# The backward key transposes of a head go to the PSUM bank of the head outputs

## The chip, the cores and the metric

The kernel runs on one core of a Trainium2 chip. The metric is the device time of one execution in microseconds (us); lower is better. Three runs of the kernel before took 1967.69, 1967.95 and 1969.16 us, so the median is 1967.95 us.

Engines are named as the profile names them: PE is the matmul engine (PEld its weight loads), DVE the vector engine, ACT the scalar engine, POOL the GpSimd engine, SP the engine that issues most DMAs. Each engine works through its own instructions in the order of the program and stands still at an instruction that has to wait for another engine.

## The reference

The reference is one layer of a bidirectional encoder over 1024 positions of width 1024, all in float32: a mixer branch with 8 heads (HGRN2, a gated linear recurrence, run forward and backward in time), a gated spatial branch, a merge of the two, and then a gated feed-forward layer and a gated residual. What matters here is the recurrence of one head and one direction:

```
def step(state, inp):
    qc, kc, vc, gc = inp                       # one chunk of positions
    b = jnp.cumsum(gc, axis=2)
    o_inter = jnp.einsum('bhtk,bhkv->bhtv', qc * jnp.exp(b), state)
    ...
    scores = jnp.einsum('bhtk,bhsk,bhtsk->bhts', qc, kc, decay)
    o_intra = jnp.einsum('bhts,bhsv->bhtv', scores, vc)
    new_state = exp(b_last) * state + einsum('bhsk,bhsv->bhkv', kc * exp(b_last - b), vc)
    return new_state, o_inter + o_intra
```

Both directions run over the same queries and values, and their outputs are added, normalised per head and gated.

## The kernel before, in words

The kernel splits the 1024 positions into 8 chunks of 128. For each of the 8 heads it does three things.

`proj` makes the forget gates and keys of a head from the normalised input, with matmuls of 512 columns in line 133 (`mm3`) that write the banks `ps_mm`. These are long and wait for little: they fill PE while a head's chains run elsewhere.

`scores` builds the score matrices of a head in seven levels, for blocks of m = 1, 2, 4, ... 64 positions, after a first product in line 613. At each level line 624 multiplies the decayed keys `X` with the decayed queries `QA` (four matmuls for each half of the positions, into a bank `ps_sc`), DVE updates `QA` (line 633) and the next `X` (line 636), line 646 or 643 merges the bank into the scores `SC`, ACT copies the middle of the next `X` from `Y` (line 657), POOL makes the next `Y` from `X` (line 660), and DVE halves the number of gate factors `F` (line 666). A level's `X` is a new tile; three buffers rotate, so the third level of a head overwrites the last `X` of the head before, and has to wait for those who still read it.

`outputs` takes the last `X` and `Y` of a head, which are the keys decayed to their chunk's borders. For two groups of chunks (4 and 3 of the 7 that pass a state on) and for both directions d (0 forward, 1 backward) it transposes the keys on PE (line 683) into a PSUM bank, copies them on ACT to the tile `kt` (line 685), multiplies them with the values (line 688, bank `ps_st`, of which there is one), and adds the products to the running states `S` on DVE (lines 692 and 694). Then line 712 computes the head's outputs into the bank `ps_o`, and line 722 transposes them into `ps_tr`.

PSUM has eight banks, given out by tags: three `mm`, two `sc`, and one each of `tr`, `st` and `o` (`PS_BUFS`, line 56). A bank that is to be written again waits until its last reader is done. Before the change all key transposes of heads 0 to 6 go to the one bank `tr`, so each of the four groups waits until ACT has copied the group before it. In the last head the backward ones go to `sc`, which is free by then.

The program is written head by head as `scores(h)`, `proj(h+1)`, `outputs(h)`, but that isn't the order in which it runs: a scheduler with a model of the engines' times sorts the instructions of each engine (`schedule_with_timeline_sim`, line 1090). So the end of the levels of head h, the transposes and states of head h, and the first levels of head h+1 are mixed on each engine. The prediction calls this stretch the passage from head h to head h+1. In the traced execution the passage from head 2 to head 3 lies at about 722 to 741 us.

Of the kernel before, what the change touches and what calls it, by code (L numbers as in the profile page):

```python
# [22 lines left out]
H = 8  # L23
# [12 lines left out]
def kernel(ctx: ExitStack, tc: tile.TileContext, a: dict, out: bass.AP):  # L36
# [18 lines left out]
    def ps_tile(tag):  # L55
        return psum.tile([P, NH], F32, name=f"ps_{tag}", tag=tag, bufs=PS_BUFS[tag])
# [16 lines left out]
    def t2(pool, role, bufs=2):  # L73
        return pool.tile([P, NH], F32, name=role, tag=role, bufs=bufs)

    def sm(role, w=1):
        return small.tile([P, w], F32, name=role, tag=role)
# [18 lines left out]
    def rstd_from(role, ssq, w, scale):  # L96

        v = sm(role + "v", w)
        nc.vector.tensor_scalar(out=v, in0=ssq, scalar1=scale, scalar2=EPS, op0=ALU.mult, op1=ALU.add)
        r = sm(role + "r", w)  # L100
        nc.gpsimd.tensor_tensor(out=r, in0=v, in1=expo[:, 0:w], op=ALU.pow)
        return r
# [10 lines left out]
    def split_into(hi, lo, src, eng=None):  # L113
        nc.scalar.activation(hi, src, AF.Copy)  # L114
        (eng or nc.vector).tensor_tensor(out=lo, in0=src, in1=hi.bitcast(F32), op=ALU.subtract)  # L115
# [339 lines left out]
    for t in range(NT):  # L455
        tp = ps_tile(("tr", "o")[t % 2])
# [213 lines left out]
    def outputs(h, s):  # L670
        QA, SC, X, Y, F, v = s.QA, s.SC, s.X, s.Y, s.F, s.v

        S = hg.tile([P, 2, NT - 1, P], F32, name="S")
        orders = [list(range(NT - 1)), list(range(NT - 1, 0, -1))]
        prev = [None, None]
        for g0 in range(0, NT - 1, 4):
            for d in range(2):
                cs = orders[d][g0:g0 + 4]
                n = len(cs)
                tp = ps_tile("sc" if h == H - 1 and d else "tr")  # L680
                for i, c in enumerate(cs):
                    src = X if c % 2 == d else Y
                    nc.tensor.transpose(tp[:, i * P:(i + 1) * P], src[:, c * P:(c + 1) * P], ident)
                kt = hg.tile([P, 4, P], F32, name="kt", bufs=2)
                nc.scalar.activation(kt[:, 0:n], tp[:, 0:n * P].rearrange("p (c t) -> p c t", c=n), AF.Copy)
                up = ps_tile("sc" if h == H - 1 and d else "st")
                for i, c in enumerate(cs):
                    nc.tensor.matmul(up[:, i * P:(i + 1) * P], lhsT=kt[:, i], rhs=v[:, c], start=True, stop=True)  # L688
                for i, c in enumerate(cs):
                    uv = up[:, i * P:(i + 1) * P]  # L690
                    if prev[d] is None:
                        nc.vector.tensor_copy(S[:, d, c - d], uv)
                    else:
                        nc.vector.scalar_tensor_tensor(
                            out=S[:, d, c - d], in0=S[:, d, prev[d] - d], scalar=F[:, 1 - d, c:c + 1], in1=uv,
                            op0=ALU.mult, op1=ALU.add)
                    prev[d] = c


        for g in range(2):  # L700
            op = ps_tile("sc" if h == H - 1 and g else "o")
            ssq = sm("os", 4)
            for i in range(4):
                c = 4 * g + i
                cs = slice(c * P, (c + 1) * P)
                terms = [(SC[:, c], v[:, c])]
                if c > 0:
                    terms.append((QA[:, 1, cs], S[:, 0, c - 1]))
                if c < NT - 1:
                    terms.append((QA[:, 0, cs], S[:, 1, c]))  # L710
                for j, (l, r) in enumerate(terms):
                    nc.tensor.matmul(op[:, i * P:(i + 1) * P], lhsT=l, rhs=r, start=(j == 0), stop=(j == len(terms) - 1))  # L712
            on = t2(t1, "on")
            for i in range(4):
                nc.scalar.activation(on[:, i * P:(i + 1) * P], op[:, i * P:(i + 1) * P], AF.Square,
                                     accum_out=ssq[:, i:i + 1])
            r = rstd_from("o", ssq, 4, 1.0 / P)
            for i in range(4):
                nc.scalar.activation(on[:, i * P:(i + 1) * P], op[:, i * P:(i + 1) * P], AF.Identity, scale=r[:, i:i + 1])
            tp = ps_tile("tr")  # L720
            for i in range(4):
                nc.tensor.transpose(tp[:, i * P:(i + 1) * P], on[:, i * P:(i + 1) * P], ident)
            gs = slice(g * NH, (g + 1) * NH)
            nc.vector.scalar_tensor_tensor(out=on, in0=tp, scalar=vec[:, 2, h:h + 1], in1=s.zg[:, gs],
                                           op0=ALU.mult, op1=ALU.mult)
            if h == H - 1:
                A = (A0, A1)[g]
                split_into(A[0][1][:, h % 4, :], A[1][1][:, h % 4, :], on)
            else:
                nc.sync.dma_start(at_d[h, :, gs], on)  # L730
# [28 lines left out]
    for h in range(H):  # L759
        nxt = Head()  # L760
        scores(h, cur)
        if h + 1 < H:
            proj(nxt, h + 1, "qfbg")
        if h == H - 1:

            gate_a(0)
            A0 = new_fm("A0")
            load_A(0, A0, range(H - 1), 5)
            gate_a(1)
            A1 = new_fm("A1")  # L770
            wa = [split_wa(load_wa(j)) for j in range(2)]
        outputs(h, cur)
        cur = nxt
# [320 lines left out]
```

## Time and profile before

| what | value |
|---|---|
| median of three runs | 1967.95 us |
| profiled execution, its own time | 1966.99 us |
| span of the profiled execution | 1965.2 us |
| PE busy | 1910.8 us, 97% of the span |
| DVE, ACT, POOL busy | 1120.0, 757.2, 206.7 us |
| share of PE in the chain that ended last | 90% |

The profiled execution was about 1 us shorter than the median. Times in the rows below are counted from the start of the span. PE is busy almost everywhere, so a shorter or longer time comes from the places where it stands idle. A row of the timeline merges equal instructions that follow each other on an engine; a float32 matmul of 128 columns appears as two.

### The profile page before, as it was taken

What the parts mean: (1) busy time and instruction counts of PE and PEld (TensorE: products, weight loads), DVE (VectorE), ACT (ScalarE), POOL (GpSimd) and SP (SyncE); (2) the same over time, 40 slices, a digit from 0 to 9 for tenths busy, and PEclk for the clock granted to TensorE, in tenths of its full rate; (3) what the DMA queues carried; (4) which work ended last, traced back from release to release, by engine and by line L of the source; (5) the groups of instructions that cost most, each with busy time, mean ns of one, the idle gap of its engine ahead of it and who ended that gap; (6) DMA issues with size and microseconds to landing.
All of it is one profiled execution on the core that took longest, in us unless ns stands there. A gap on an engine that the chain in (4) does not pass through costs nothing.

```text
span 1965.2 us, 24005 instructions
## 1 busy us (share of the span) xinstructions
PE 1910.8 (97%) x9264; PEld 1596.0 (81%) x9264; DVE 1120.0 (57%) x1712; ACT 757.2 (39%) x1424; POOL 206.7 (11%) x153
## 2 busy tenths in 40 slices
PE   7999999999999999999989998999999999999999
PEld 6887888888887888888877887888888888888887
DVE  7402385544348777777665468855554537545743
ACT  6312254343354545545441356433333324112321
POOL 2600000000012222222112100000000000001000
PEclk9999999999999999999999999999999999999999
DMA  7220245323231221212336333232222106315222
GB/s 292 93 88 27 87 172 170 130 105 110 86 123 33 70 71 63 66 55 68 126 106 208 107 99 103 97 112 78 89 76 86 65 33 209 108 65 163 92 102 79
DMA packets 82690, 201.86 MB, mean 103 GB/s; under 512 B 8720, under 2 KB 18064, under 8 KB 82576
## 3 DMA queue, kind: packets, MB, share of 16 engines
q1 hardware_dynamic: 82576, 200.33, 30.2%
q8 instruction: 73, 1.20, 0.3%
q14 instruction: 41, 0.34, 0.0%
HBM read 147.35 MB, written 52.95 MB: 102 GB/s over the span
## 4 chain that ended last, share of the span: by engine, by line
PE 90%; DVE 4%; ACT 2%; DMA 2%; POOL 1%; issue 1%; SPq 0%; DVEq 0%; POOLq 0%; ACTq 0%
PE ps_mm L133 29%; PE ps_mm L278 20%; PE ps_sc L133 11%; PE ps_sc L278 10%; PE ps_st L133 6%; PE ps_sc L624 4%; PE ps_o L278 2%; PE ps_o L712 2%; PE ps_tr L278 2%; PE ps_st L278 1%; DVE QA L633 1%; POOL Y L660 1%; PE ps_st L688 1%; ACT SC L643 0%; DMA raw<-in_w_gate_dram 0%
## 5 line engine op out<-in xcount | busy, mean ns | idle before, releaser
L278 PE MATMUL ps_mm<-T,w 128*128 128x512 f32 x1296 | 309.6, 389 | 0.0
L278 PEld LDWEIGHTS ps_mm<-T,w 128*128 128x128 f32 x1296 | 243.2, 188 | 50.7 <-ACT u L228 0.2
L115 DVE TENSOR_TENSOR whl<-raw,whl 128x1024 fp32r<-128x1024 f32 (+1 forms) x70 | 89.6, 1282 | 142.7 <-ACT whl L114 142.6
L660 POOL TENSOR_TENSOR Y<-X,F 128x512 f32<-128x512 f32 x56 | 92.4, 1651 | 696.1 <-DVE F L599 392.4
L624 PE MATMUL ps_sc<-QA,X 128*128 128x128 f32 x896 | 126.4, 288 | 16.9 <-DVE QA L633 16.9
L115 DVE TENSOR_TENSOR w<-sums,w 128x1024 fp32r<-128x1024 f32 x72 | 88.0, 1223 | 94.2 <-ACT w L114 94.2
L624 PEld LDWEIGHTS ps_sc<-QA,X 128*128 128x128 f32 x896 | 116.1, 192 | 26.1 <-DVE QA L633 19.0
L133 PE MATMUL ps_mm<-whl,act 128*128 128x512 f32 x528 | 134.1, 389 | 0.0
L114 ACT ACTIVATE whl<-raw 128x1024 fp32r<-128x1024 f32 (+1 forms) x78 | 79.1, 1017 | 120.2 <-PE ps_sc L133 52.4
L633 DVE TENSOR_TENSOR QA<-QA,F 128x512 f32<-128x512 f32 x112 | 91.8, 828 | 49.2 <-PE ps_sc L624 48.1
L133 PE MATMUL ps_mm<-hTb,whl 128*128 128x512 f32 x480 | 118.6, 396 | 0.0
L133 PEld LDWEIGHTS ps_mm<-whl,act 128*128 128x128 f32 x528 | 99.1, 188 | 20.7
L133 PE MATMUL ps_mm<-hTa,whl 128*128 128x512 f32 x480 | 115.1, 392 | 0.0
L114 ACT ACTIVATE w<-sums 128x1024 fp32r<-128x1024 f32 x72 | 75.9, 1055 | 99.9 <-PE ps_sc L278 76.9
L278 PE MATMUL ps_sc<-T,w 128*128 128x512 f32 x432 | 107.5, 389 | 0.0
L133 PEld LDWEIGHTS ps_mm<-hTa,whl 128*128 128x128 f32 x480 | 89.4, 188 | 18.1
L133 PEld LDWEIGHTS ps_mm<-hTb,whl 128*128 128x128 f32 x480 | 88.2, 188 | 16.8
L278 PEld LDWEIGHTS ps_sc<-T,w 128*128 128x128 f32 x432 | 81.1, 188 | 16.9
L133 PE MATMUL ps_sc<-whl,act 128*128 128x512 f32 x354 | 91.0, 390 | 0.3 <-ACT acc L953 0.3
L133 PEld LDWEIGHTS ps_sc<-whl,act 128*128 128x128 f32 x354 | 66.3, 188 | 14.3 <-ACT acc L953 0.7
L115 POOL TENSOR_TENSOR wpg<-raw,wpg 128x1024 fp32r<-128x1024 f32 x4 | 9.6, 2403 | 598.3 <-ACT wpg L114 593.6
L278 PE MATMUL ps_mm<-B,wA 128*128 128x512 f32 x264 | 67.3, 399 | 1.7 <-ACT wA L114 1.7
(309 smaller groups left out, 3574.2 us busy)
## 6 DMA issues: line engine op xcount, KB each, us to landing
raw<-in_w_fm_dram SPq DMA_DIRECT2D x52, 512.0 KB, 3.6
raw<-in_w_gate_dram SPq DMA_DIRECT2D x22, 512.0 KB, 3.4
raw<-in_w_up_dram SPq DMA_DIRECT2D x22, 512.0 KB, 3.9
act_d<-s SPq DMA_DIRECT2D x22, 512.0 KB, 2.8
raw<-in_w_down_dram SPq DMA_DIRECT2D x22, 512.0 KB, 4.4
raw<-act_d SPq DMA_DIRECT2D x22, 512.0 KB, 4.2
raw<-in_w_tm_dram SPq DMA_DIRECT2D x16, 512.0 KB, 4.1
pr_d<-vs SPq DMA_DIRECT2D x16, 256.0 KB, 5.9
```

The costliest lines, as they stand in the source:

```text
L114: nc.scalar.activation(hi, src, AF.Copy)
L115: (eng or nc.vector).tensor_tensor(out=lo, in0=src, in1=hi.bitcast(F32), op=ALU.subtract)
L133: nc.tensor.matmul(ps, lhsT=lhs(lp, k), rhs=rhs(rp, k), start=(i == 0), stop=(i == n - 1))
L278: nc.tensor.matmul(ps, lhsT=lhs(lp, k), rhs=rhs(rp, k), start=(first and i == 0), stop=(i == n - 1), skip_group_check=True)
L624: nc.tensor.matmul(sp[:, i * P:(i + 1) * P], lhsT=X[:, c * P:(c + 1) * P], rhs=view(QA, c * P, [[2 * m, cb], [T + m, 2], [1, m]]), start=T ...
L633: nc.vector.tensor_tensor(out=view(QA, o, qd), in0=view(QA, o, qd), in1=view(F, of + 1, [[nb - 1, 2], [2, nb // 4], [0, m]]), op=ALU.mult)
L660: nc.gpsimd.tensor_tensor(out=view(Y, m, mid), in0=view(X, m, mid), in1=view(F, 0, [[4, nb // 4], [nb + 3, 2], [0, m]]), op=ALU.mult)
L688: nc.tensor.matmul(up[:, i * P:(i + 1) * P], lhsT=kt[:, i], rhs=v[:, c], start=True, stop=True)
L712: nc.tensor.matmul(op[:, i * P:(i + 1) * P], lhsT=l, rhs=r, start=(j == 0), stop=(j == len(terms) - 1))
```

## The change

One line of `outputs` picks the bank of the key transposes by direction. The forward transposes stay in `tr`; the backward ones go to `o`, or in the last head to `sc` as before.

```
@@ -677,7 +677,7 @@
             for d in range(2):
                 cs = orders[d][g0:g0 + 4]
                 n = len(cs)
-                tp = ps_tile("sc" if h == H - 1 and d else "tr")
+                tp = ps_tile(("tr", "sc" if h == H - 1 else "o")[d])
                 for i, c in enumerate(cs):
                     src = X if c % 2 == d else Y
                     nc.tensor.transpose(tp[:, i * P:(i + 1) * P], src[:, c * P:(c + 1) * P], ident)
```

No instruction is added or removed, but the scheduler puts many of them elsewhere. On PE, in the passage from head 2 to head 3, from the second half of the product of line 613 (`ps_sc_5409`) to the first level of head 3 (`ps_sc_5416` and `ps_sc_5424` are its two halves), this is the order before:

```order
L613 MATMUL ps_sc_5409<-q_5126,ks_5399 128x128 [waits PE_49,Activation_49]
L613 MATMUL ps_sc_5409<-q_5126,ks_5399 128x128 x3
L683 MATMUL ps_tr_5306<-ident_79,X_5103 128x128 [waits Activation_49]
L683 MATMUL ps_tr_5306<-ident_79,Y_4686 128x128
L683 MATMUL ps_tr_5306<-ident_79,X_5103 128x128
L688 MATMUL ps_st_5297<-v_4827,kt_5295 128x128 [waits DVE_49]
L688 MATMUL ps_st_5297<-v_4827,kt_5295 128x128 x3
L624 MATMUL ps_sc_5416<-QA_5398,X0_5129 128x128 [waits Activation_49]
L624 MATMUL ps_sc_5416<-QA_5398,X0_5129 128x128 x3
L683 MATMUL ps_tr_5319<-ident_79,X_5103 128x128 [waits Activation_49]
L683 MATMUL ps_tr_5319<-ident_79,Y_4686 128x128
L683 MATMUL ps_tr_5319<-ident_79,X_5103 128x128
```

And this is the order now, at the same place:

```order
L613 MATMUL ps_sc_5409<-q_5126,ks_5399 128x128 [waits PE_49,Activation_49]
L613 MATMUL ps_sc_5409<-q_5126,ks_5399 128x128 x3
L688 MATMUL ps_st_5297<-v_4827,kt_5295 128x128 [waits DVE_49]
L688 MATMUL ps_st_5297<-v_4827,kt_5295 128x128 x3
L624 MATMUL ps_sc_5416<-QA_5398,X0_5129 128x128 [waits Activation_49]
L624 MATMUL ps_sc_5416<-QA_5398,X0_5129 128x128 x3
L712 MATMUL ps_o_5332<-v_4827,SC_4956 128x128 [waits Activation_49]
L624 MATMUL ps_sc_5424<-QA_5398,X0_5129 128x128 [waits DVE_49]
L624 MATMUL ps_sc_5424<-QA_5398,X0_5129 128x128 x3
```

The six transposes that stood among these matmuls now stand ahead of line 613, and the first matmul of line 712, which needs the bank `o` free again, has moved behind the first half of the level. What is left between line 613 and the first level is the state product `ps_st_5297`, which waits for DVE.

On DVE, at the same passage, the order before is this (`X_5436` and `X_5457` are the second and third new `X` of head 3, `ps_st_5281` the first state product of head 2):

```order
L636 TENSOR_TENSOR X_5436<-X_5415,F2_5434 128x64x2x2 [waits DVE_49]
L666 TENSOR_TENSOR F64_5545<-F32_5518 128x32 [waits DVE_49]
L692 COPY S_5273<-ps_st_5281 128x128 [waits PE_49]
L666 TENSOR_TENSOR F128_5568<-F64_5545 128x16 [waits DVE_49]
L694 SCALAR_TENSOR_TENSOR S_5273<-S_5273,F128_5124,ps_st_5281 128x128 [waits DVE_49] x3
L692 COPY S_5273<-ps_st_5297 128x128 [waits PE_49]
```

And this is the order now:

```order
L636 TENSOR_TENSOR X_5436<-X_5415,F2_5434 128x64x2x2 [waits DVE_49]
L666 TENSOR_TENSOR F64_5545<-F32_5518 128x32 [waits DVE_49]
L692 COPY S_5273<-ps_st_5281 128x128 [waits PE_49]
L636 TENSOR_TENSOR X_5457<-X_5436,F4_5455 128x32x2x4 [waits DVE_49,PE_49,Activation_49]
L636 TENSOR_TENSOR X_5457<-X_5436,F4_5455 128x32x2x4 [waits DVE_49]
L666 TENSOR_TENSOR F128_5568<-F64_5545 128x16 [waits DVE_49]
L694 SCALAR_TENSOR_TENSOR S_5273<-S_5273,F128_5124,ps_st_5281 128x128 [waits DVE_49] x3
L692 COPY S_5273<-ps_st_5297 128x128 [waits PE_49]
```

The pair of line 636 that makes the third `X` of the next head has moved from behind the first update of `QA` (line 633, further down) to ahead of the three state updates of line 694. It reads `X_5436`, whose middle ACT writes (line 657). On ACT the second copy `kt` of a head now follows the first at once, the fourth has moved behind the two copies of line 614, and so has line 657 of the third level moved ahead of them. POOL's and SP's orders are the same. These moves are the same at the passages from heads 0 to 5; at the passage from head 6 to head 7, where the last projection matmuls lie between the levels, they are spread over a longer stretch.

## Rows read from the trace of the kernel before

**Rows 1.** The page's first line.

```profile
span 1965.2 us, 24005 instructions
```

**Rows 2.** Waits on PE, 610 to 1025 us: waiter, releaser, total us, times, longest.

```profile
PE ps_tr L683 <- ACT kt L685: 6.5, 5, 1.3
```

**Rows 3.** Timeline, 718 to 742 us: start, length, engine, line, operation, [idle before <-releaser].

```profile
727.19 4.13 POOL L660 TENSOR_TENSOR Y<-X,F 128x512 f32<-128x512 f32 x1 [3.37 <-ACT X L657]
...
728.87 0.75 DVE L636 TENSOR_TENSOR X<-X,F 128x256 f32<-128x256 f32 x2
...
729.35 1.87 PEld L613 LDWEIGHTS ps_sc<-q,ks 128*128 128x128 f32 x16
...
729.54 1.83 DVE L666 TENSOR_TENSOR F<-F 128x32 f32<-128x32 f32 x1
731.29 0.28 DVE L692 COPY S<-ps_st 128x128 f32<-128x128 f32 x1
731.35 0.67 ACT L657 ACTIVATE X<-Y 128x512 f32<-128x512 f32 x1 [2.17 <-POOL Y L660]
...
731.61 1.11 DVE L694 SCALAR_TENSOR_TENSOR S<-S,F,ps_st 128x128 f32<-128x128 f32 x3
732.04 0.60 ACT L685 ACTIVATE kt<-ps_tr 128x512 f32<-128x512 f32 x1
732.10 1.50 POOL L660 TENSOR_TENSOR Y<-X,F 128x512 f32<-128x512 f32 x1 [0.78 <-ACT X L657]
...
732.69 0.14 PEld L683 LDWEIGHTS ps_tr<-ident,X 128*128 128x128 f32 x1 [1.47 <-ACT kt L685]
...
732.97 0.97 PEld L688 LDWEIGHTS ps_st<-v,kt 128*128 128x128 f32 x8
...
733.86 1.29 PEld L624 LDWEIGHTS ps_sc<-QA,X 128*128 128x128 f32 x8
...
735.50 0.69 DVE L633 TENSOR_TENSOR QA<-QA,F 128x512 f32<-128x512 f32 x1 [0.27 <-PE ps_sc L624]
...
736.24 1.28 PEld L624 LDWEIGHTS ps_sc<-QA,X 128*128 128x128 f32 x8 [0.70 <-DVE QA L633]
...
737.64 1.27 POOL L660 TENSOR_TENSOR Y<-X,F 128x512 f32<-128x512 f32 x1 [4.05 <-ACT X L657]
...
737.87 1.59 DVE L633 TENSOR_TENSOR QA<-QA,F 128x512 f32<-128x512 f32 x1
...
739.52 1.02 PEld L624 LDWEIGHTS ps_sc<-QA,X 128*128 128x128 f32 x8 [1.21 <-DVE QA L633]
...
740.47 1.69 PEld L133 LDWEIGHTS ps_mm<-hTb,whl 128*128 128x128 f32 x8
```

**Rows 4.** Timeline of POOL, 660 to 900 us: first and last of five like this.

```profile
674.33 4.13 POOL L660 TENSOR_TENSOR Y<-X,F 128x512 f32<-128x512 f32 x1 [3.36 <-ACT X L657]
...
885.74 4.20 POOL L660 TENSOR_TENSOR Y<-X,F 128x512 f32<-128x512 f32 x1 [3.36 <-ACT X L657]
```

**Rows 5.** Timeline, 620 to 635 us, the passage from head 0 to head 1.

```profile
624.01 1.80 POOL L660 TENSOR_TENSOR Y<-X,F 128x512 f32<-128x512 f32 x1 [0.79 <-ACT X L657]
624.37 1.49 DVE L666 TENSOR_TENSOR F<-F 128x32 f32<-128x32 f32 x1
...
627.26 0.97 PEld L688 LDWEIGHTS ps_st<-v,kt 128*128 128x128 f32 x8 [1.84 <-DVE S L694]
```

**Rows 6.** Timeline of PEld at three other places with long idle times.

```profile
34.36 1.23 PEld L133 LDWEIGHTS ps_mm<-wp,pT 128*128 128x128 f32 x6 [2.40 <-DVE vs L405]
...
1017.86 0.91 PEld L722 LDWEIGHTS ps_tr<-ident,on 128*128 128x128 f32 x4 [3.11 <-ACT on L719]
...
1209.27 0.42 PEld L846 LDWEIGHTS ps_tr<-ident,y 128*128 128x128 f32 x4 [3.21 <-issue]
```

**Rows 7.** Windows: stretch, us, busy of PE, PEld, DVE, ACT, POOL, granted clock, DMA.

```profile
1019.60:1022.90 3.30, 3.00 (x9) 2.57 (x10) 2.44 (x5) 1.65 (x4) 0.00 (x0) 0.50 0.00 0
...
1210.70:1217.40 6.70, 5.32 (x12) 3.92 (x13) 5.93 (x9) 5.16 (x12) 0.00 (x0) 0.50 0.30 85
```

More of the change, by code (lines that the diff above doesn't have):

```diff
@@ L679, in outputs @@
                 n = len(cs)
-                tp = ps_tile("sc" if h == H - 1 and d else "tr")
+                tp = ps_tile(("tr", "sc" if h == H - 1 else "o")[d])
                 for i, c in enumerate(cs):
```

## The prediction

> **What bounds the kernel now.** I read the page first. The span is 1965.2 us [rows 1] and PE is busy nearly all of it, so only PE's idle places can change the time. Next I read the waits of PE over the heads. The wait that the change aims at is there: a transpose of line 683 waits for ACT's copy to `kt`, 5 times, 6.5 us in all, never above 1.3 us [rows 2]. Those five are the passages from heads 1 to 5. Last I read the timeline of one passage, from head 2 to head 3, engine by engine [rows 3].
>
> The chain in it runs like this. POOL's op of line 660 is issued at 727.19 and takes 4.13 us. DVE works without a pause beside it until 729.62 (the pair of line 636), and then DVE's next op, a tiny one of line 666, takes 1.83 us; both end together, at 731.32 and 731.37. ACT's copy of line 657 needs that `Y` and starts at 731.35. Behind it in ACT's order stands the second copy to `kt`, at 732.04. PE has been through with line 613 since about 731.14 (two loads per 0.223 us, 16 loads from 729.35) and stands until 732.69, when the bank `tr` is free. Then come three transposes, the state product (732.97), the first half of the next head's first level (733.86), DVE's update of `QA` (735.50), the second half (736.24), the second update (737.87 to 739.46) and the first half of the second level (739.52). From 740.47 the long matmuls of line 133 run and PE has no more such gaps until the next passage. So a delay of the matmul at 739.52 is a delay of the whole program, once per passage.
>
> **What the change takes away.** The third and fourth group of transposes no longer wait for ACT's second `kt`, which now stands ahead of POOL's long op. They go into the idle time ahead of line 613; ten transposes at some 0.11 us are hidden there and cost nothing. If nothing else stood in the way, the state product could follow line 613 at 731.14, where it starts at 732.97: at most 1.83 us per passage, 9.2 us over five.
>
> **What is late next.** The state product writes the only bank `st`, and has to wait for the three updates of line 694 that read the product before. In the trace these run 731.61 to 732.72, right behind lines 692 and 666. In the new order the pair of line 636 stands between, and that pair reads the `X` whose middle ACT writes at 731.35 to 732.02. DVE, with everything behind it, waits for that copy:
>
> - the pair starts at about 732.05 and takes 0.75, as at 728.87, so the next op on DVE is issued at 732.72 (issues overlap by 0.08);
> - the next POOL op is issued at 732.10, in the middle of the pair. A small op of line 666 behind a pair of line 636 with POOL's op pending took 1.83 us [rows 3] and 1.49 us at head 0, where POOL was issued at 624.01 and DVE at 624.37 [rows 5]. I take 1.49: line 666 ends at about 734.2;
> - the three updates take 1.11: 735.3. PE follows 0.05 behind, as at 627.26, where it waited for just this [rows 5]: the state product starts at 735.35 instead of 732.97, 2.38 us later.
>
> From there the old steps, taken from start to start: 0.89 to the level's first half (736.24), 1.64 to DVE's update (737.88), 0.69 and 0.05 to the second half (738.62), 1.63 to the second update (740.25). That update took 1.59 us in the trace where the first took 0.69, because POOL's third op was issued 0.23 us ahead of it, at 737.64. Now POOL's third op follows ACT's copy of the third level, which has moved up to about 734.8, so it is over by then; I give the second update 0.69, and it ends at 740.94 instead of 739.46. The passage becomes 1.48 us longer: 2.38 lost at the state product, 0.90 got back at the second update.
>
> The bounds of this step: if line 666 doesn't lose to POOL, the updates start at 732.83 and the state product could run at 734.0. But ACT's order now has three activations and the copy of the third level ahead of line 614, which frees the bank for the first level, so that half starts at about 735.2 to 735.5, and the passage is 0.4 to 0.7 us longer. If DVE loses the 1.83 in full, it is 1.8 us longer. I take 1.48, since at heads 1 to 5 POOL's op is the same one (4.13 to 4.20 us, five times [rows 4]): 5 x 1.48 = 7.4 us.
>
> On the pair of DVE and POOL the Trainium skill (SBUF — State Buffer, section on the two separate sides) says that a GpSimd op and a DVE op with two SBUF inputs exclude each other for a whole instruction and that the one that starts first goes first. The 1.59 against 0.69 agrees; the 4.13 does not quite, since DVE started five ops while POOL waited. Without the exclusion the sum would be 5 x 0.4 = 2.0 us, with it 7.4.
>
> At head 0 the state product already waits for line 694 [rows 5], and POOL's ops there end early enough that the pair finds its input ready. It adds its own 0.75 us, or 0.9 with what the longer ACT queue adds; against that stands the 0.90 got back. I cost that passage at nothing. From head 6 to head 7 matmuls of line 133 lie between all these steps; moving them costs PE nothing as long as some are left to run, so nothing, plus or minus 0.5 us.
>
> **PE's clock.** The new wait on PE is 731.14 to 735.35, 4.2 us in one piece, where 1.55 stood. Two waits in the trace come near it, of 3.11 and 3.21 us [rows 6], and behind both the granted clock fell to 0.50, so from 2.4 to 1.2 GHz, for at least 3.3 and 6.7 us [rows 7]. After a wait of 2.40 us, at 34.36, no such stretch follows. So I expect falls here too. What lies on PE's part of the chain right behind the wait is 0.89 + 1.28 = 2.17 us of full-speed work; at half speed all of it would cost 2.2 us more, and a fall that comes late or is over early costs nothing. I take 1.2 us, at three passages of five: 3.6 us. Bounds: 0 and 5 x 2.2 = 11.
>
> The Trainium skill (TensorE: Matmul & The Clock Gate, section on HAM oscillation) tells of a loop whose waits between bursts let the clock fall anew in every round. By that rule it falls at all five.
>
> **Sum.** 7.4 + 3.6 = 11.0 us longer. Against the profiled execution's own 1966.99 us that is 1978; the median of the runs, 1967.95, is 1 us above that execution, so I predict 1979 us for the median.
>
> **Rivals.**
>
> - *The clock falls at all five passages and stays down over the whole piece:* 7.4 + 11 = 18.4, 1986 us. For it speak the two waits that were shorter and sufficed; against it that PE works densely before and behind this one.
> - *POOL isn't in DVE's way:* 0.4 to 0.7 us per passage and a wait on PE under 3 us, with no fall of the clock: 2 to 3.5 us, 1970 to 1971.5. For it speaks that POOL's second op took only 1.50 us with the three updates of line 694 beside it [rows 3]; both ops of line 666 in the rows speak against.
> - *Faster: POOL's first op gets through early.* If it takes its turn as soon as the op of DVE ends that runs when it is issued, as the page's rule would have it, DVE loses the same 1.7 us, but earlier: it still reaches line 692 at about 731.3, while ACT's copy is done long before. Then the pair doesn't wait, the updates end 0.75 us later than they did, and the state product starts at about 733.5, 0.55 late; with the 0.90 got back at the second update a passage is 0.35 us shorter. If the pair also falls into a time in which DVE had nothing to do, it is the whole 0.90. So 1.7 to 4.5 us less, 1963.5 to 1966. It decides from the point where the state product starts before 733.87. Against it: DVE's order up to there is unchanged, PE's added transposes fall into a wait, and the long op of POOL stood in five passages of five [rows 4].
> - *Nothing moves:* the wait for `kt` goes, one of equal length takes its place, the order later in the head gives back the rest: within 2 us of 1968.
>
> **How the numbers follow.** My forecast has 0.51, the clock at all five 0.15, no POOL conflict 0.13, faster 0.13, nothing 0.08. A difference of 0.2% (3.9 us) is about what can be told from none. Slower by more than that are the first two and a little of the third, 0.68; within it are most of the third, a third of the fourth and most of the fifth, 0.22; faster is the rest, 0.10. The forecast's own range is 1974 (no fall, 1.2 us per passage) to 1987. Over all, 1966 to 1987 leaves out most of the faster case and some of the largest falls, about 2 in 10.
>
> **What would show it.** In the profile after, line 683 no longer waits for `kt`, and in five passages PE's line 688 waits some 4 us for line 694; on DVE the pair of line 636 starts right behind an ACT copy of line 657, and line 666 behind it takes over 1.4 us; the second update of `QA` takes 0.7 instead of 1.59. The distance from passage to passage, (885.74 - 674.33) / 4 = 52.85 us now [rows 4], grows to 54.3 or more. The clock shows new stretches at 0.5 behind those waits. I am wrong if line 694 is done before 733 in the picture of the old times, or if the 4.13 us op of POOL is gone.

## The result, and the profile after

The changed kernel took 1981.99 us (median of 6 runs, 1979.04 to 1985.05) against 1969.11 us of the kernel before in the same session (6 runs, 1967.69 to 1969.39). The ratio is 1.0066, 95% interval 1.0053 to 1.0079: 12.9 us slower, where 11 were forecast. The profiled execution took 1982.70 us.

The page's first line, beside [rows 1]:

```profile
span 1980.9 us, 24012 instructions
```

The seven instructions more are not among the work of the engines: PE runs 9264, DVE 1712, ACT 1424 and POOL 153 in both profiles.

The waits on PE between 610 and 1030 us (waiter, releaser, us in total, times, longest). In the kernel before there stood, beside [rows 2]:

```profile
PE ps_sc L624 <- DVE QA L633: 16.1, 24, 1.5
...
PE ps_st L688 <- DVE S L694: 1.6, 1, 1.6
```

And in the changed kernel:

```profile
PE ps_st L688 <- DVE S L694: 21.9, 6, 3.9
PE ps_sc L624 <- DVE QA L633: 9.5, 18, 1.5
```

The wait of line 683 for `kt` is gone, all five times. In its place line 688 waits for line 694, six times and 21.9 us in all, where 6.5 us stood at line 683 and 1.6 us (at head 0) at line 688. Line 624's wait for `QA` shrank from 16.1 to 9.5 us: that is the part given back.

The timeline of the changed kernel at the passage that [rows 3] shows (start, length, engine, line, operation, count, idle time before it and its releaser):

```profile
733.77 4.12 POOL L660 TENSOR_TENSOR Y<-X,F 128x512 f32<-128x512 f32 x1 [3.37 <-ACT X L657]
...
734.38 0.97 PEld L688 LDWEIGHTS ps_st<-v,kt 128*128 128x128 f32 x8
...
735.93 1.86 PEld L613 LDWEIGHTS ps_sc<-q,ks 128*128 128x128 f32 x16
...
736.12 1.83 DVE L666 TENSOR_TENSOR F<-F 128x32 f32<-128x32 f32 x1
737.87 0.28 DVE L692 COPY S<-ps_st 128x128 f32<-128x128 f32 x1
737.93 0.66 ACT L657 ACTIVATE X<-Y 128x512 f32<-128x512 f32 x1 [1.68 <-POOL Y L660]
...
738.62 2.06 DVE L636 TENSOR_TENSOR X<-X,F 128x256 f32<-128x256 f32 x2 [0.47 <-ACT X L657]
738.66 1.74 POOL L660 TENSOR_TENSOR Y<-X,F 128x512 f32<-128x512 f32 x1 [0.77 <-ACT X L657]
...
740.61 0.16 DVE L666 TENSOR_TENSOR F<-F 128x16 f32<-128x16 f32 x1
740.69 1.10 DVE L694 SCALAR_TENSOR_TENSOR S<-S,F,ps_st 128x128 f32<-128x128 f32 x3
...
741.84 1.78 PEld L688 LDWEIGHTS ps_st<-v,kt 128*128 128x128 f32 x8 [4.05 <-DVE S L694]
...
743.50 1.83 PEld L624 LDWEIGHTS ps_sc<-QA,X 128*128 128x128 f32 x8
...
746.41 1.64 PEld L624 LDWEIGHTS ps_sc<-QA,X 128*128 128x128 f32 x8 [0.65 <-DVE QA L633]
...
748.39 0.69 DVE L633 TENSOR_TENSOR QA<-QA,F 128x512 f32<-128x512 f32 x1 [1.17 <-PE ps_sc L624]
...
749.13 1.02 PEld L624 LDWEIGHTS ps_sc<-QA,X 128*128 128x128 f32 x8 [0.31 <-DVE QA L633]
```

Read it from the first state product of the head. In the kernel before it stands at 727.80:

```profile
727.80 0.97 PEld L688 LDWEIGHTS ps_st<-v,kt 128*128 128x128 f32 x8
```

Here it stands at 734.38, so 6.58 us are taken off to compare. The pair of line 636 starts right behind ACT's copy, at 732.04 in old times, and takes 2.06 us beside POOL's op. The three updates of line 694 start at 734.11 and PE's state product at 735.26 (predicted: 735.35). Its eight loads take 1.78 us instead of 0.97, because the clock has fallen. The second update of `QA` takes 0.69 us instead of 1.59.

POOL's long op, the first and the last of five, beside [rows 4]:

```profile
678.20 4.21 POOL L660 TENSOR_TENSOR Y<-X,F 128x512 f32<-128x512 f32 x1 [3.35 <-ACT X L657]
...
899.49 4.20 POOL L660 TENSOR_TENSOR Y<-X,F 128x512 f32<-128x512 f32 x1 [3.37 <-ACT X L657]
```

The distance from passage to passage is (899.49 - 678.20) / 4 = 55.32 us, 2.47 more than before; this is the mean of the passages from heads 1 to 4. Windows behind those waits (stretch, us, busy time and count of PE, PEld, DVE, ACT, POOL, then the granted clock and DMA):

```profile
631.80:635.20 3.40, 3.16 (x16) 2.87 (x14) 1.61 (x5) 0.64 (x2) 0.00 (x0) 0.50 0.00 0
686.40:689.80 3.40, 3.40 (x16) 3.40 (x17) 0.98 (x3) 1.46 (x4) 0.53 (x1) 0.50 0.00 0
741.00:747.80 6.80, 5.60 (x24) 5.31 (x25) 3.26 (x9) 2.35 (x6) 1.27 (x1) 0.50 0.00 1
```

Three more like the first two follow, at 799.1, 853.7 and 908.3: the clock is at 0.50, so at 1.2 GHz, behind all six waits.

The two profiled spans differ by 15.7 us, and 3.5 of these are there already at the first state product of the first passage (625.24 against 621.73), behind a fall of the clock near 37.9 us that other kernels here show or don't show, with the old bank as with the new. The passage from head 0 adds 0.4 us, four times 2.47 make 9.9, and from the last of POOL's ops to the end it is 1.9 us, in which the passages from heads 5 and 6 lie. From the first state product of head 5 to that of head 7 it is 120.31 us against 118.17, so these two passages together cost 2.1 us; seven matmuls of line 133 have moved from the one to the other, so their lengths can't be compared one by one. So the change costs about 12.2 us in the trace, which agrees with the medians.

### The profile page after: what moved, and what is told of

Its sections match the earlier page's. It is cut to its first block, busy times and chain, and to the rows that moved or that the text cites. A ratio compares the mean times of both kernels' runs of the same rounds, so it can differ in the third digit from the quotient of the medians.

```text
span 1980.9 us, 24012 instructions
## 1 busy us (share of the span) xinstructions
PE 1920.7 (97%) x9264; PEld 1606.1 (81%) x9264; DVE 1113.5 (56%) x1712; ACT 756.9 (38%) x1424; POOL 206.6 (10%) x153
## 4 chain that ended last, share of the span: by engine, by line
PE 91%; DVE 4%; ACT 2%; DMA 1%; POOL 1%; issue 1%; SPq 0%; DVEq 0%; POOLq 0%
PE ps_mm L133 30%; PE ps_mm L278 19%; PE ps_sc L133 11%; PE ps_sc L278 10%; PE ps_st L133 6%; PE ps_sc L624 5%; PE ps_o L278 2%; PE ps_o L712 2%; PE ps_tr L278 2%; PE ps_st L278 1%; POOL Y L660 1%; PE ps_st L688 1%; DVE X L636 1%; DVE QA L633 1%; ACT SC L643 0%
## 5 line engine op out<-in xcount | busy, mean ns | idle before, releaser
L633 DVE TENSOR_TENSOR QA<-QA,F 128x512 f32<-128x512 f32 x112 | 84.4, 762 | 53.7 <-PE ps_sc L624 53.2
L636 DVE TENSOR_TENSOR X<-X,F 128x256 f32<-128x256 f32 x112 | 71.1, 670 | 9.4 <-ACT X L657 9.2
```

What stands on the lines that cost most here:

```text
L633: nc.vector.tensor_tensor(out=view(QA, o, qd), in0=view(QA, o, qd), in1=view(F, of + 1, [[nb - 1, 2], [2, nb // 4], [0, m]]), op=ALU.mult)
L636: nc.vector.tensor_tensor(out=view(X2, o, dims), in0=view(X, o, dims), in1=view(F, nb + of + 1, [[4, nb // 8], [1 - nb, 2], [0, m]]), op=A ...
```

## The experiments

Nine kernels; each was timed five or eleven times beside the kernel before, whose medians were 1968.2 to 1968.9 us. Added lines shift the line numbers; each section says what they are. The rows shown are of the passage from head 2 to head 3; the length of "the passage" is the distance of POOL's long ops, from first to last of the five, divided by four, so a mean over heads 1 to 4. Orders were changed with a helper that queues one instruction behind another on the same engine and adds no wait:

```
+    def behind(i, name):
+        if name in marks:
+            tc.add_manual_dep(i.ins, marks[name].ins.name, ...)
```

### The pair back behind line 694

```
                 nc.vector.tensor_tensor(out=view(X2, o, dims), ...
+                if m == 4:
+                    behind(x, ("S", h - 1))
```

> The changed kernel, but with the pair of line 636 (third level) queued on DVE behind the three state updates of line 694 instead of ahead of them; ACT's, PE's and POOL's orders are as in the changed kernel. Theory (the pair's place in DVE's order costs the time): in the passages between heads the state product of line 688 starts about 2.4 us earlier than in the changed kernel, but the first half of the next head's first level is then bound by ACT's late copy of line 614, so a passage is 0 to 0.4 us longer than in the kernel before; the wait on PE is about 2 us and the clock does not fall there: 1968 to 1973 us. Rival (the shared bank itself, or the transposes' new place on PE, costs the time): it stays at 1979 to 1983 us.

Measured: 1973.8 us, ratio 1.0028 (1.0018 to 1.0037). This is 8 us less than the changed kernel, and 5.6 us above the one before, just outside what was expected. Its trace (line 704 is 694, 644 is 636, 698 is 688, 632 is 624, 622 is 614):

```profile
726.97 0.97 PEld L698 LDWEIGHTS ps_st<-v,kt 128*128 128x128 f32 x8
...
730.78 1.11 DVE L704 SCALAR_TENSOR_TENSOR S<-S,F,ps_st 128x128 f32<-128x128 f32 x3
...
731.95 0.97 PEld L698 LDWEIGHTS ps_st<-v,kt 128*128 128x128 f32 x8 [1.56 <-DVE S L704]
...
734.08 1.28 PEld L632 LDWEIGHTS ps_sc<-QA,X 128*128 128x128 f32 x8 [1.16 <-ACT SC L622]
```

The state product follows 4.98 us behind the first one (726.97) where it took 5.17 before and 7.46 in the changed kernel, and the first level then waits for ACT's copy, both as expected. The passage is 53.37 us, 0.51 above the kernel before, where 0 to 0.4 were expected. That the clock would stay up was wrong. The profiled execution is the fastest of eleven, at a mean clock of 0.994, and even there a window of the passage shows the fall:

```profile
737.10:740.40 3.30, 3.30 (x18) 3.30 (x18) 2.17 (x5) 1.29 (x3) 0.00 (x0) 0.52 0.00 0
```

The other ten ran at 0.987 to 0.991 and took 1971.2 to 1978.4 us. So DVE's order explains more than half of the loss, 7.3 of 12.9 us, and the clock still falls in some of the passages. In the profiled execution it fell at those from heads 2, 3 and 5. Behind the same two waits of 1.56 and 1.16 us it did not fall at head 4.

### The pair and ACT's copies

The same, and on ACT:

```
             nc.scalar.activation(view(X2, m, mid), view(Y, m, mid), AF.Copy)
+            if m == 4:
+                behind(x, ("SC", h))          # SC: the last copy of line 614
...
                     nc.scalar.activation(dst[...], sv[:, :, par], AF.Identity, scale=om)
+                    if par != d:
+                        behind(x, ("SC", h - 1))
```

> As the run with the pair queued behind line 694, and also with the two copies of line 614 queued on ACT ahead of the third level's copy of line 657 and of two writes to Y of line 596. Theory: both things that are late behind the change are gone, the state product starts about 1.1 to 1.8 us earlier in a passage than in the kernel before and nothing behind it waits for ACT: five passages give 3 to 7 us, 1961 to 1966 us, faster than both kernels. Rival (what ACT does later, the copies of line 657 above all, is late instead and DVE's second update of QA loses to POOL again): within 3 us of the kernel before, 1966 to 1972. Rival (the shared bank costs the time): 1979 to 1983.

Measured: 1962.1 us, ratio 0.9974 (0.9966 to 0.9983): the theory's time, faster than both kernels. The passage is 51.95 us. The first level now follows the state product at once (line 624 is the copy of 614, 702 is 688, 634 is 624, 643 is 633):

```profile
732.78 1.08 ACT L624 ACTIVATE SC<-ps_sc 128x512 f32<-128x512 f32 x2
...
733.13 0.97 PEld L702 LDWEIGHTS ps_st<-v,kt 128*128 128x128 f32 x8 [1.56 <-DVE S L708]
...
734.02 1.30 PEld L634 LDWEIGHTS ps_sc<-QA,X 128*128 128x128 f32 x8
...
738.19 0.69 DVE L643 TENSOR_TENSOR QA<-QA,F 128x512 f32<-128x512 f32 x1 [0.77 <-PE ps_sc L634]
```

There is no fall of the clock in the passages. One part of the theory was off: the state product is only 0.2 us earlier than before here, and 0.2 to 0.5 us over heads 1 to 5, not 1.1 to 1.8; the gain is in the main the second update, which no longer meets POOL.

### PE kept busy through the wait

```
-            for i in range(4):
+            for i in list(range(4)) * (4 if g and h else 1):      # the matmuls of line 613
```

> The changed kernel, with the second group of matmuls of line 613 done four times over from head 1 on (same values into the same bank), which fills 2.7 us of PE's wait for line 694 in each passage and moves no other instruction. Theory (lateness of line 694 and a fall of the clock behind the wait, both): no stretch at 0.50 in the passages from head 1 on, the steps behind the state product at full speed, 0.8 to 1.4 us less per passage than the changed kernel, 1974 to 1979 us. Rival (the clock falls only beside other waits and costs nothing): 1981 to 1984. Rival (the clock carries nearly all of it): 1968 to 1972. If the added matmuls were themselves in the way it would be slower than the changed kernel, about 1985 to 1995.

Measured: 1977.0 us, ratio 1.0050 (1.0036 to 1.0063). The interval overlaps with that of the changed kernel, so the trace has to decide. Its passage:

```profile
732.10 4.54 PEld L613 LDWEIGHTS ps_sc<-q,ks 128*128 128x128 f32 x40
...
734.81 2.07 DVE L636 TENSOR_TENSOR X<-X,F 128x256 f32<-128x256 f32 x2 [0.49 <-ACT X L657]
...
738.05 0.97 PEld L688 LDWEIGHTS ps_st<-v,kt 128*128 128x128 f32 x8 [1.40 <-DVE S L694]
...
743.69 1.02 PEld L624 LDWEIGHTS ps_sc<-QA,X 128*128 128x128 f32 x8 [0.31 <-DVE QA L633]
```

The pair and the state product are as late as in the changed kernel (7.50 us behind the first product at 730.55; 7.46 there), the clock is at 1.00 from 600 to 960 us, and POOL's long ops lie at:

```profile
675.58 4.21 POOL L660 TENSOR_TENSOR Y<-X,F 128x512 f32<-128x512 f32 x1 [3.36 <-ACT X L657]
...
892.81 4.21 POOL L660 TENSOR_TENSOR Y<-X,F 128x512 f32<-128x512 f32 x1 [3.35 <-ACT X L657]
```

That is 54.31 us: 1.46 above the kernel before, 1.01 below the changed one. The two parts stand apart: 1.46 us of lateness, 1.01 us of clock (0.61 to 1.60 in the four passages). The time as a whole shows less of it, since the passage from head 6 to head 7, where PE has little idle time to fill, is 1.2 us longer with the added matmuls (59.10 us from first state product to first state product, 57.88 in the changed kernel).

### POOL's op at m = 4 left out

```
-            nc.gpsimd.tensor_tensor(out=view(Y, m, mid), ...
+            if m != 4:
+                nc.gpsimd.tensor_tensor(out=view(Y, m, mid), ...
```

> The changed kernel without POOL's op of line 660 at the third level (m = 4): Y is not updated there, so the outputs differ; all other orders are those of the changed kernel. It takes away what the pair of line 636 collides with, and leaves the pair where it is and its wait for ACT's copy. Theory (the pair of 2.06 us loses 1.3 us to POOL): the pair takes 0.75 us, the state product starts 1.3 us earlier, the wait on PE is about 2.9 us, a passage is 1.3 to 2 us shorter than in the changed kernel: 1972 to 1976 us. Rival (the pair is late only because its input is late, and what looks like a collision is that wait): 1980 to 1983, and the pair still takes over 1.5 us.

Measured: 1979.7 us, ratio 1.0064 (1.0051 to 1.0076): no change against the changed kernel that is clear of noise; the passage is 55.28 us (55.32 there), and the pair's rows stay as they were:

```profile
734.39 2.06 DVE L636 TENSOR_TENSOR X<-X,F 128x256 f32<-128x256 f32 x2 [0.47 <-ACT X L657]
734.44 1.73 POOL L661 TENSOR_TENSOR Y<-X,F 128x512 f32<-128x512 f32 x1 [0.76 <-ACT X L657]
```

The pair is as long as the rival said, and the time is 0.3 us below the rival's range, but not by its reason: I had left out the wrong op. The one beside the pair, which is DVE's work of m = 4, is POOL's of m = 2. The run serves as a control: leaving out an op of POOL's that doesn't lie beside the pair leaves the passage as it was.

### POOL's op at m = 2 left out

The same edit with `m != 2`.

> The changed kernel without POOL's op of line 660 at m = 2: Y is not updated there, so the outputs differ. The run without the op at m = 4 took away the wrong one: the op that runs beside the pair of line 636 is the one at m = 2, which starts at 738.66 in the changed kernel's trace. POOL's op of 4.1 us at m = 1, and with it the wait of the pair for ACT's copy, stay. ACT's second copy of line 614 moves up by two places with it. Theory (the pair of 2.06 us loses 1.3 us to POOL): the pair takes 0.75 us, the state product starts about 1.3 us earlier, PE's wait is about 2.8 us instead of 4.1, a passage is 1.3 to 2.3 us shorter than the 55.3 us of the changed kernel: 1970 to 1976 us. Rival (no collision; the pair's length has another cause): the pair still takes over 1.5 us, passages stay at 55.3 us, 1979 to 1983 us.

Measured: 1971.7 us, ratio 1.0014 (1.0005 to 1.0023), the passage 53.90 us. Its rows (line 689 is 688):

```profile
734.40 0.76 DVE L636 TENSOR_TENSOR X<-X,F 128x256 f32<-128x256 f32 x2 [0.47 <-ACT X L657]
...
736.32 1.73 PEld L689 LDWEIGHTS ps_st<-v,kt 128*128 128x128 f32 x8 [2.75 <-DVE S L695]
```

The pair waits for ACT as before and takes 0.76 us, and the product comes 6.16 us behind the first one (730.16) instead of 7.46: 1.30 us earlier. So the collision is real, and the theory holds in each number. The pair's 0.76 us shows it by itself; the time as a whole also holds what else the edit moves, ACT's second copy of line 614 and the op left out in every head. The clock still falls behind waits of 2.74 to 2.83 us at the passages from heads 1 to 4, but not behind 2.74 at head 5.

### The same orders with the old bank

The kernel before with the edits of the run of 1962.1 us, the transposes left in `tr`.

> The kernel before (backward transposes in the bank tr) with the same edits to the orders as the run with the pair and the copies of line 614 moved, which took 1962.1 us. It asks what the bank brings once the orders are right. Theory (the gain there lies in the orders, since the state product then waits for line 694 in either kernel): 1962 to 1966 us, the passage 52.0 to 52.6 us. Rival (the bank brings it, the wait for kt being what holds the state product): 1967 to 1970 us, the passage 52.8 us as in the kernel before.

Measured: 1968.6 us, ratio 0.9999 (0.9990 to 1.0007), the passage 52.84 us. The rival holds: with these orders the bank makes the whole gain. The wait for `kt` stands as in [rows 2], and the second update of `QA` (line 643) meets POOL again:

```profile
PE ps_tr L697 <- ACT kt L699: 6.4, 5, 1.3
```

```profile
739.58 1.27 POOL L674 TENSOR_TENSOR Y<-X,F 128x512 f32<-128x512 f32 x1 [4.05 <-ACT X L669]
739.80 1.60 DVE L643 TENSOR_TENSOR QA<-QA,F 128x512 f32<-128x512 f32 x1
```

ACT stands 1.72 us for PE's last transposes into `tr` here, and behind that, and behind the last copy `kt`, comes the copy that releases POOL. With the transposes in `o` this copy comes first, and POOL's op is under way (734.69 to 735.97) before the second update starts at 738.19.

### The updates ahead of line 666

In the changed kernel, besides the copies of line 614 moved ahead of line 657 of m = 2 (and, as above, of the two writes of line 596) and the pair of m = 4 behind the first update of `QA`:

```
             nc.vector.tensor_tensor(out=F2, in0=Fv[:, :, :, 0], in1=Fv[:, :, :, 1], op=ALU.mult)
+            if m >= 32:
+                behind(x, ("S", h - 1))
```

> The changed kernel with more moved: the small products of line 666 for F64 and F128 behind the three updates of line 694, the pair of line 636 at m = 4 behind the first update of QA (line 633), and ACT's copies of line 614 ahead of the copy of line 657 at m = 2. Theory (in the run of 1962.1 us the state product still waits 1.56 us for line 694, which is late because the op of line 666 ahead of it loses 1.6 us to POOL; lines 692 and 694 read PSUM and do not lose): the state product follows line 613 at once, 1.0 to 1.4 us per passage, 1955 to 1958 us. Rival (line 692 or 694 now loses to POOL in place of line 666): 1960 to 1964 us. Rival (ACT's later copy of line 657 delays POOL's chain and with it the second update of QA): 1963 to 1970 us.

Measured: 1956.7 us, ratio 0.9939 (0.9926 to 0.9951): the theory's time. In its rows line 710 is 692, 712 is 694, 682 is 666, 706 is 688:

```profile
728.58 0.97 PEld L706 LDWEIGHTS ps_st<-v,kt 128*128 128x128 f32 x8
...
730.33 0.28 DVE L710 COPY S<-ps_st 128x128 f32<-128x128 f32 x1
...
730.64 1.11 DVE L712 SCALAR_TENSOR_TENSOR S<-S,F,ps_st 128x128 f32<-128x128 f32 x3
...
731.67 0.68 DVE L682 TENSOR_TENSOR F<-F 128x32 f32<-128x32 f32 x2
...
731.92 0.97 PEld L706 LDWEIGHTS ps_st<-v,kt 128*128 128x128 f32 x8
...
737.91 0.74 PEld L706 LDWEIGHTS ps_st<-v,kt 128*128 128x128 f32 x6 [1.06 <-DVE S L712]
```

POOL's long op stands from 727.97 to 732.08, and lines 692 and 694 lose nothing beside it. The state product follows the first one (728.58) by 3.34 us, against 5.17 before, and doesn't wait. A new wait of 1.06 us stands at the head's last state product instead. So the passages from heads 2 to 4 are 51.13 us, 0.8 shorter than in the run of 1962.1 us, where 1.0 to 1.4 were expected; of the 5.4 us between the two traces 3.6 lie in the passages from heads 5 and 6 together (113.64 against 117.21 us from the first state product of head 5 to that of head 7).

### The updates first, old bank

> The kernel before (backward transposes in the bank tr) with the edits to the orders of the run with line 666 behind line 694. Theory (with line 694 early, the wait of the transposes for the second kt is what the state product waits for, and the bank's change would pay): with ACT's copies of kt no longer behind line 657 most of that wait is gone too, 1957 to 1962 us, 1 to 4 us slower than the same orders with the changed bank. Rival (the bank brings nothing in any order): within 1 us of the same orders with the changed bank. Rival (the bank was the whole gain): 1967 to 1970 us.

Measured: 1959.9 us, ratio 0.9951 (0.9937 to 0.9965). The median is 3.1 us above that of the same orders with the new bank, as the theory had it, but the intervals overlap. Its second `kt` (line 703) follows PE at once, and the wait that the change was to take away is gone without a change of bank:

```profile
728.95 0.60 ACT L703 ACTIVATE kt<-ps_tr 128x512 f32<-128x512 f32 x1 [0.27 <-PE ps_tr L701]
...
730.98 0.97 PEld L706 LDWEIGHTS ps_st<-v,kt 128*128 128x128 f32 x8
```

Its passages are 51.39 us, against 51.13 in the last three of the kernel with the new bank (the first of its four, with a fall of the clock, is 52.67). Between the two traces, which are 2.5 us apart, the difference lies in the passages from heads 5 and 6: from the first state product of head 5 to that of head 7 it is 116.11 us here and 113.64 with the new bank.

### One copy earlier

The fastest kernel with the copy of line 657 at m = 2 between the two copies of line 614.

> The fastest kernel so far (1956.7 us: line 666 behind line 694, the pair at m = 4 behind the first update of QA, ACT's copies of line 614 ahead of the copy of line 657 at m = 2), with that copy of line 657 now between the two copies of line 614 instead of behind both. Theory (the first update of QA still takes 1.06 us instead of 0.69 because POOL's op at m = 2 starts only at 733.46, a microsecond after its input could be there): the copy and POOL's op come 0.6 us earlier, the first update no longer meets POOL, 0.3 to 0.5 us per passage, 1954 to 1956 us. Rival (the second copy of line 614, now later, holds the second half of the first level): 1957 to 1960 us. Rival (POOL's next op meets the pair all the same, and the second update is what ends last): no change, 1956 to 1958 us.

Measured: 1957.1 us, ratio 0.9942 (0.9928 to 0.9955): no change, the last rival. The first update takes 0.69 us, as hoped, but then the pair (line 646) meets POOL's next op and takes 1.76:

```profile
734.29 1.28 POOL L676 TENSOR_TENSOR Y<-X,F 128x512 f32<-128x512 f32 x1 [1.19 <-ACT X L671]
```

```profile
734.42 1.76 DVE L646 TENSOR_TENSOR X<-X,F 128x256 f32<-128x256 f32 x2
```

## Why the prediction was right

- **The wait that goes, and what is late next.** Right: the wait for `kt` went, and line 694 was what PE waited for at all five passages (and at head 0, as before). With the pair back behind line 694, the product came 2.5 us earlier again.
- **Lateness, 7.4 us.** Forecast: the product 2.38 us later, 0.90 back at the second update, 1.48 per passage. In the run with the clock held up: 7.50 - 5.17 = 2.33 later, 0.91 back (6.55 us from the product to the second level in the kernel before, 738.05 to 743.69 = 5.64 there), 1.46 from passage to passage, a mean over heads 1 to 4; taken for head 5 too, 7.3 us over five.
- **Which op loses to POOL.** Wrong in detail: I let the pair pass in 0.75 us and line 666 lose 1.49. The pair itself lost 1.3 us and the 666 behind it took 0.16. The sign that line 666 would take over 1.4 us failed. The sum of the two came out the same, 2.2 us; I read this as DVE having to let one op of POOL's through either way, but no run tests it, and the 1.49 that I took was of another place, so the size is in part luck.
- **The clock, 3.6 us.** Under-sized. I took 1.2 us at three passages; it fell at all five and at head 0, and cost 1.01 us on average over heads 1 to 4: 5.0 us over five. The rival that let it fall at all five had the number of falls right and its price, 2.2 us, too high: the four passages cost 0.61 to 1.60 us. Five of the six stretches at 0.50 lasted some 3.4 us, and in the longest PE was busy for 5.60 us of 6.80.
- **Head 0, nothing.** It cost 0.4 us, with a wait of 2.58 us and a fall of the clock behind it. The lateness alone didn't cost anything there: with the clock held up, it is 52.79 us from the first state product of head 0 to that of head 1, against 53.21 in the kernel before and 53.59 in the changed one.
- **The sum.** 7.3 + 5.0 + 0.4 = 12.7 against 11.0 forecast; the medians say 12.9, the traces 12.2. The 1.7 us above the forecast are the clock and head 0. The fifth passage is taken to be like the four that were measured: with it at 2.47 us, the passage from head 6 to head 7 comes out at -0.3, within the forecast's plus or minus 0.5.
- **The rivals.** That POOL isn't in DVE's way is refuted by the run without the op at m = 2, which brought 1.30 us per product; the 10 us that it brought in all also hold clock and what else that edit moved. The faster case asked for a POOL op that gets through early; its length stayed at 4.12 to 4.21 us in all five. Something in the bank was worth having all the same, 6 us in the run with both orders moved, but only with an order that the scheduler did not choose.

## What to carry to other kernels

Freeing a bank changes the order that a scheduler writes, and that order is the change: compare it engine by engine before counting the wait that goes. When one wait on the bounding engine goes, ask what its next instruction waits for, and whether the instructions ahead of that on another engine's queue are needed so soon; here two small products that nobody waited for held the state product back by 1.4 to 1.6 us at each passage (4.71 to 4.98 us behind the first one, against 3.34). What a bank that is free earlier is worth depends on the orders: 12.9 us lost with the scheduler's, 6 us won with the first set of moved orders, and with the second set 3.1 us, which is not clear of noise.

## What the runs showed of the hardware that was not expected

In the run with the updates first, DVE's ops that read PSUM and at most one SBUF tensor (lines 692 and 694) took 0.28 and 1.11 us, as elsewhere, while POOL's op was pending and, for part of the time, under way: it ended at 732.08, and the shortest of its kind over the heads take 1.06 us, while line 694 ran until 731.75. A product of two SBUF tensors of 32 columns took 1.83 at that place in the kernel before.

The length of PE's waits didn't decide by itself whether the clock fell. It fell behind 2.58 us at head 0 of the changed kernel, and in the run with the updates first at one passage (head 1) whose longest wait was 1.05 us, but not at the next four, with the same wait of 1.06. With the pair moved back it fell behind 1.56 and 1.16 us at two passages and not at a third. In [rows 6] and [rows 7] it fell behind 3.11 and 3.21 us and not behind 2.40. What else decides, no run here shows. With the pair moved back, the same program ran at a mean clock of 0.987 in one execution and 0.994 in another, 7.6 us apart.
